# Experts in quarters of 32 slots, residual ahead of the last weights, tail two tiles ahead: one mixer and MoE layer on one core

## The chip, the cores and the metric

The kernel runs on one core of one Trainium2 chip. The metric is device time in microseconds (us). The kernel before takes 887.61 us, the median of three runs (886.54 to 891.98). Engines are named PE (matrix multiplication), DVE (vector), ACT (activation), POOL (which also issues the gathers and scatters) and SP (which issues the plain loads and stores).

## The reference

One layer: a token mixer (a state-space branch and a convolution branch), then a mixture of 32 experts, of which each of the 512 tokens takes two, then a last norm. The change touches the experts and the end.

```python
D_MODEL, SEQ, N_EXPERTS, TOP_K, D_EXPERT = 1024, 512, 32, 2, 256
...
weights = jax.nn.softmax(top_logits, axis=-1) * p_group          # two experts for a token
gate = jnp.sum(jax.nn.one_hot(expert_id, N_EXPERTS) * weights[..., None], axis=1)
out = jnp.zeros_like(h)
for e in range(N_EXPERTS):
    act = jax.nn.silu(h @ w_gate[e]) * (h @ w_up[e])             # 512x1024 @ 1024x256, twice
    out = out + gate[:, e:e + 1] * (act @ w_down[e])             # 512x256 @ 256x1024
...
x = x + gt2 * out
return rmsnorm(x, g_final)
```

## The kernel before

Until 561 us the kernel runs the mixer and the router. What the router leaves are index tables: for each expert up to 128 slots with the rows of its tokens, and the class of its size (16, 32, 48, 64, 96 or 128 slots, `SIZES`). The inputs are fixed, and so are the counts. Worked out from the reference, 20 of the 32 experts have at most 32 tokens ("small" below), 8 have 33 to 64 (11, 12, 13, 22, 24, 25, 28, 30: "middle"), and 4 have more (8, 9, 14, 15: "big").

**Expert by expert.** For each expert POOL gathers its rows (L1318) out of DRAM into `xg`, PE turns them (`tile_x`, L1329) into `st`, multiplies them by the gate and up weights (`tile_gu`, L1346, result `peg`), ACT and DVE form silu(gate) times up (`tile_act`, `sge`), PE turns that (`tile_at`, L1358, `pat`), ACT copies it (`at`), PE multiplies it by the down weights (`tile_down`, L1366, `ped`), DVE scales it by `gt2` into `ye` (`tile_y`, L1376; two buffers, used in turn), and POOL scatters `ye` to DRAM rows `ybuf` (`scatter_h`, L1401).

**Two column tiles.** Slots are worked in halves of 64, and gate and up lie on two column tiles of the array, 64 columns each: the gate of slots in partitions 0 to 63 and up in 64 to 127. The second half of the slots stands behind an If (`halves`) that is taken where the expert has more than 64 tokens. So a small or middle expert has 32 matmuls of 128x256 for gate and up and 8 of 128x512 for down, and a big one 64 and 16, as the trace counts them (two for each matmul in the code).

**Order.** The order on PE, ACT and DVE is that of the code. Step e of the loop issues on PE: gate and up of e, the turn `pat` of e-1, the turn `pxt` of the rows of e+1, down of e-1. Then DVE forms y of e-1 and POOL scatters it. POOL's order is set by the scheduler: gather of e+4, scatter of e, gather of e+5, and so on.

**Scatters.** A scatter of an expert is declared free of the scatters of the experts before it, which write other rows:

```python
    ins = halves(more[e], lambda a: scatter_h(e, a, y))
    for i_ in ins:
        for p_ in scattered:
            tc.declare_no_dep(...)          # reason="rows of different experts"
    scattered.extend(ins)
```

Nothing is declared between the scatters of one expert, so the second half's waits until the first's has landed.

**Weights.** SP loads 1 MB thirds of an expert (gate, up, down; `load_p`, `part_load`) through a ring of 20 pieces, and the loop asks for them six to seven experts ahead. Behind the last weights come the residual `x1` (2 MB) and the last gain (`last_loads`, L1507 and L1510).

**The end.** Experts 30 and 31 aren't scattered: their results are brought to the token rows by one-hot matmuls (`last_own`, L1581). The other results come back from `ybuf` (`yr`, L1565). For each of four tiles of 128 tokens `last_mix` weighs the two rows of a token (ACT, then DVE, L1586) and adds them on PE (L1588) to the residual that `last_x` (L1574) put there; then come the sum of squares on ACT, the root, the last norm on DVE (L1603) and the store. `last_mix` runs one tile ahead of the norm.

Of the kernel before, what the change touches and what calls it, by code (L numbers as in the profile page):

```python
# [2 lines left out]

# [23 lines left out]
def hybrid_kernel(  # L27
# [1240 lines left out]
    def indices(pt, p, n, name):  # L1268

        em = mz2.tile([128, 2, n], F32, tag="ixe", name=name + "_e", bufs=1)[0:p]  # L1270
        t = mz2.tile([128, 2, n], F32, tag="ixs", name=name + "_s", bufs=1)[0:p]
        V.tensor_copy(t, pt)
        V.tensor_scalar(em[:, 0], t[:, 0], 0.0, BIG, op0=ALU.is_equal, op1=ALU.mult)
        V.scalar_tensor_tensor(em[:, 1], t[:, 1], 128.0, t[:, 0], op0=ALU.mult, op1=ALU.add)
        V.scalar_tensor_tensor(em[:, 1], em[:, 0], -1.0, em[:, 1], op0=ALU.add, op1=ALU.add)
        ix = mz2.tile([p, 2, n], I32, tag="ix" + name, name=name)
        V.tensor_copy(ix[:, 1], em[:, 1])
        V.tensor_scalar(em[:, 0], em[:, 1], float(L), -float(L), op0=ALU.is_ge, op1=ALU.mult)
        V.tensor_tensor(ix[:, 0], em[:, 0], em[:, 1], op=ALU.add)
        if name == "tb":  # L1280

            pq = ps_tp("pixh")
            for a in range(2):
                for c in range(2):
                    T.matmul(pq[64 * c:64 * c + 64, n * a:n * a + n], lhsT=ident[:, 64 * a:64 * a + 64], rhs=em[:, 1], start=True, stop=True, skip_group_check=True)
            V.tensor_scalar(ixh.rearrange("p a e -> p (a e)"), pq[:, 0:2 * n], 2.0, cofs, op0=ALU.mult, op1=ALU.add)
        return ix

    ixh = mz2.tile([128, 2, NE], I32, name="ixh")
    pt = ps_tp("ptab")  # L1290
    n = 0
# [48 lines left out]

    H = [slice(64 * c, 64 * c + 64) for c in range(2)]

    def tile_gu(pg, st, r, a):
        for k in range(KD):
            for c in range(2):
                T.matmul(pg[H[c], 256 * a:256 * a + 256], lhsT=st[:, k, H[a]], rhs=r[c][k // 4][:, 256 * (k % 4):256 * (k % 4) + 256], start=(k == 0), stop=(k == KD - 1), skip_group_check=True)  # L1346

    def tile_act(pg):
        sg = mo.tile([128, 512], F32, tag="sge", name="sge", bufs=2)
        S.activation(sg[64:128], pg[0:64], AF.Silu)  # L1350
        V.tensor_tensor(sg[64:128], pg[64:128], sg[64:128], op=ALU.mult)
        return sg

    def tile_at(sg):
        pa = ps_tp("pat")[:, 0:256]
        for k in range(2):
            for a in range(2):
                T.transpose(pa[:, 128 * k + 64 * a:128 * k + 64 * a + 64], sg[64:128, 256 * a + k:256 * a + 256:2], ident[64:128, 64:128])  # L1358
# [4 lines left out]
    def tile_down(pd, at, r, a):  # L1363
        for k in range(2):
# [7 lines left out]
    def tile_y(pd):  # L1372

        y = new_y()
        for a in range(2):
            V.tensor_tensor(y[:, 512 * a:512 * a + 512], pd[a], gt2h, op=ALU.mult)  # L1376
        return y
# [22 lines left out]
    def scatter_h(e, a, y):  # L1400
        return G.indirect_dma_start(out=ybuf.rearrange("r (c n) -> (r c) n", c=2), out_offset=bass.IndirectOffsetOnAxis(ap=ixh[:, a, e:e + 1], axis=0),  # L1401
                                    in_=y[:, 512 * a:512 * a + 512], in_offset=None, bounds_check=4 * L - 1, oob_is_err=False)
# [8 lines left out]
    def scatter_e(e, y):  # L1411
        ins = halves(more[e], lambda a: scatter_h(e, a, y))
# [12 lines left out]
    with tc.If(n_gen > 0):  # L1425
        with tc.For_i(0, n_gen, 1):
# [56 lines left out]
            sg = mo.tile([128, 512], F32, tag="sge", name="sge", bufs=2)[:, 0:256]  # L1483
# [12 lines left out]
            yg = new_y()  # L1496
            for h in range(2):
                V.tensor_tensor(yg[:, 512 * h:512 * h + 512], pd[h], gt2[:, 512 * h:512 * h + 512], op=ALU.mult)
# [5 lines left out]
    def last_loads():  # L1504
        for h in range(2):
            t = eraw("x1").rearrange("p (i d) -> p i d", i=2)
            SY.dma_start(out=t, in_=x1d[256 * h:256 * h + 256].rearrange("(i p) d -> p i d", p=128))  # L1507
            x1s.append(t)
        x1s.append(eraw("gfin")[:, 0:1024])
        SY.dma_start(out=x1s[2], in_=g_final.rearrange("(o d) -> o d", o=1).to_broadcast([128, D]))  # L1510
# [34 lines left out]
    def last_y(pd, j):  # L1545

        y, parts = new_y(), eraw("yp").bitcast(F32R)
        g_ = last["gs"][:, j:j + 1]
# [27 lines left out]
    def last_own(j, parts):  # L1576

        for i in range(NT):
# [4 lines left out]
    def last_mix(i):  # L1583
        y = yrs[i][:, 0]
        S.activation(y, y, AF.Copy, scale=pw[:, i, 0:1])
        V.scalar_tensor_tensor(y, yrs[i][:, 1], pw[:, i, 1:2], y, op0=ALU.mult, op1=ALU.add)  # L1586
        for h in range(2):
            T.matmul(fin[i][h], lhsT=ident, rhs=y[:, 512 * h:512 * h + 512], start=False, stop=True, skip_group_check=True)  # L1588
# [25 lines left out]
    pgs = [ps_s5(f"peg{i}") for i in range(2)]  # L1614
    pd = [ps_mm(f"ped{i}") for i in range(2)]
    fin[0] = [ps_mm(f"fin{i}") for i in range(2)]
    with tc.manual_schedule(engines=MAN):
        for t in pgs + pd:
            V.memset(t, 0.0)
# [8 lines left out]
        for e in range(NE + 1):  # L1628
            gather_e(e + NXG)
            if e == NE - 3:  # L1630
                last_loads()
            if e > 0:
                sg = tile_act(pgs[(e - 1) % 2])
            if e < NE:
                halves(wide[e], lambda a: tile_gu(pgs[e % 2], st[e], eraws[e], a))
            load_wide(e + 1)
            if e == NE:
                last_x(0)
            if e > 0:
                at = tile_at(sg)  # L1640
            if e == NE:
                fin[1], fin[2] = pgs, [ps_tp(f"fin2{i}") for i in range(2)]
                last_x(1)
                last_x(2)
                last["y", 0] = last_y(pd, 0)
# [6 lines left out]
            if e > 0:  # L1652
                halves(wide[e - 1], lambda a: tile_down(pd, at, eraws[e - 1], a))
            if 0 < e < NE - 1:
# [16 lines left out]
        fin[3] = pd  # L1671
        last_x(3)
        for j in range(2):
            last_own(j, last["y", j])
        last_mix(0)
        for i in range(NT):
            if i + 1 < NT:
                last_mix(i + 1)
# [35 lines left out]
```

## Time and profile before

| | |
|---|---|
| median of 3 runs | 887.61 us (886.54 to 891.98) |
| the profiled execution | 891.78 us, of it a span of 890.1 |
| mixer and router | to 561 us |
| experts | 561 to 840 us (gate and up of expert 31 begin at 839.56) |
| end | from there to 890.1 us |
| granted clock of PE, mean | 0.943 |

The profile is of one execution. All durations below come from it, and it was 4.2 us slower than the median. Its time was 1.7 us above its span.

### The profile page before, as it was taken

Reading aid. Unit: us, or ns where it says so; the run is one execution under the profiler, and the core shown is the slowest. Engines: PE = TensorE matmul, PEld = TensorE weight load, DVE = VectorE, ACT = ScalarE, POOL = GpSimd, SP = SyncE. Lnnn points to the kernel's source line nnn. Section 1 sums busy time; section 2 is a strip of 40 time slices with the busy share of each in tenths; the row PEclk is TensorE's granted clock in tenths of the full one; section 3 lists DMA queues with packets and bytes.
Section 4 is the critical chain, followed back from the end, with each engine's and each line's share of the span. In section 5 each row is a group of like instructions: output and inputs, shape, how many; then the busy total and the mean of one; then the engine's idle time right before and its main releaser. Section 6 shows DMA issues by size and latency. Waiting matters only on the chain. (4 is left out here: it accounts for less than half of the span.)

```text
span 890.1 us, 14314 instructions
## 1 busy us (share of the span) xinstructions
PE 746.9 (84%) x5486; PEld 519.6 (58%) x5486; DVE 465.8 (52%) x723; ACT 321.7 (36%) x559; POOL 331.7 (37%) x293
## 2 busy tenths in 40 slices
PE   3598976988889997779999993788998988888895
PEld 0476853665566775646778872455655655555542
DVE  4948464564387797826875576133223123233254
ACT  3443611353555766637732330222112112212133
POOL 4657435343576788631610122122123122122400
PEclk9998996998988999999999996799999999999997
DMA  8926860341145546478687447999989998997042
GB/s 310 263 61 177 206 214 20 107 125 30 57 135 172 169 129 182 130 248 303 210 299 274 151 132 313 397 380 364 377 321 388 407 350 342 387 389 261 27 178 94
DMA packets 84678, 202.01 MB, mean 227 GB/s; under 512 B 12859, under 2 KB 42621, under 8 KB 74866
## 3 DMA queue, kind: packets, MB, share of 16 engines
q1 hardware_dynamic: 76754, 180.00, 57.3%
q0 software_dynamic: 5856, 12.45, 4.0%
q10 hardware_dynamic: 1984, 8.44, 3.5%
q8 instruction: 53, 0.87, 0.4%
q14 instruction: 31, 0.25, 0.1%
HBM read 180.16 MB, written 26.69 MB: 232 GB/s over the span
## 5 line engine op out<-in xcount | busy, mean ns | idle before, releaser
L1346 PE MATMUL peg<-eraw,st 128*64 128x256 f32 x1152 | 133.7, 386 | 9.5 <-PEq L1407 7.4
L1346 PEld LDWEIGHTS peg<-eraw,st 128*64 128x64 f32 x1152 | 94.7, 139 | 60.4 <-issue 34.8
L1331 DVE COPY st<-pxt 128x512 f32<-128x512 f32 x32 | 22.1, 692 | 160.0 <-PE pxt L1329 160.0
L1360 ACT ACTIVATE at<-pat 128x256 f32<-128x256 f32 x32 | 12.3, 384 | 215.8 <-PE pat L1358 215.8
L1318 POOL DMA_INDIRECT xg<-h2d,tb x32 | 30.4, 950 | 141.3 <-PE pxt L1329 129.6
L396 PE MATMUL zp<-hh,zuwh 128*128 128x512 f32 x192 | 78.7, 410 | 0.0
L398 PE MATMUL zp<-hh,zuwl 128*128 128x512 f32 x192 | 77.1, 401 | 0.5 <-POOL zuwl L752 0.3
L397 PE MATMUL zp<-hl,zuwh 128*128 128x512 f32 x192 | 76.8, 400 | 0.0
L1366 PE MATMUL ped<-eraw,at 128*64 128x512 f32 x288 | 68.9, 603 | 0.0
L98 POOL TENSOR_TENSOR adacc<-adacc,wa 128x512 f32<-128x512 f32 x30 | 47.1, 1570 | 39.9 <-ACT wa L854 37.6
L1376 DVE TENSOR_TENSOR ye<-ped,gt2h 128x512 f32<-128x512 f32 x60 | 39.0, 687 | 40.2 <-PE ped L1366 37.3
L1401 POOL DMA_INDIRECT ybuf<-ye,ixh x34 | 34.0, 999 | 69.5 <-DVE ye L1376 49.8
L1329 PE MATMUL pxt<-ident,xg 128*128 128x128 f32 x256 | 42.4, 303 | 8.1 <-DMA xg<-h2d,tb 7.4
L396 PEld LDWEIGHTS zp<-hh,zuwh 128*128 128x128 f32 x192 | 37.4, 195 | 11.9 <-issue 4.4
L398 PEld LDWEIGHTS zp<-hh,zuwl 128*128 128x128 f32 x192 | 37.2, 194 | 9.8 <-POOL zuwl L752 1.8
L397 PEld LDWEIGHTS zp<-hl,zuwh 128*128 128x128 f32 x192 | 37.1, 193 | 7.4
L1329 PEld LDWEIGHTS pxt<-ident,xg 128*128 128x128 f32 x256 | 33.6, 194 | 13.1 <-issue 8.6
L1358 PE MATMUL pat<-ident,sge 64*128 64x64 f32 x128 | 21.3, 286 | 18.9 <-PEq L1407 18.2
L1358 PEld LDWEIGHTS pat<-ident,sge 64*128 64x128 f32 x128 | 17.7, 209 | 32.7 <-PEq L1407 30.4
L1366 PEld LDWEIGHTS ped<-eraw,at 128*64 128x64 f32 x288 | 17.8, 136 | 27.2 <-issue 23.6
L98 POOL TENSOR_TENSOR vb<-vta,vtb 128x512 f32<-128x512 f32 x16 | 22.3, 1393 | 30.0 <-PE pv L533 19.1
L752 DVE TENSOR_TENSOR zuwl<-zr,zuwh 128x1024 fp32r<-128x1024 f32 x16 | 28.4, 1775 | 5.7 <-ACT zuwh L751 5.6
(494 smaller groups left out, 1666.9 us busy)
## 6 DMA issues: line engine op xcount, KB each, us to landing
eraw<-in_w_exp_gate_dram SPq DMA_DIRECT2D x24, 1024.0 KB
eraw<-in_w_exp_up_dram SPq DMA_DIRECT2D x24, 1024.0 KB
eraw<-in_w_exp_down_dram SPq DMA_DIRECT2D x24, 1024.0 KB
wa<-in_w_ada_dram SPq DMA_DIRECT2D x32, 512.0 KB
zr<-in_w_in_dram SPq DMA_DIRECT2D x12, 1024.0 KB
wa<-in_w_ada_dram SPq DMA_DIRECT2D x8, 1024.0 KB
eraw<-in_w_exp_gate_dram SPq DMA_DIRECT2D x14, 512.0 KB
eraw<-in_w_exp_down_dram SPq DMA_DIRECT2D x14, 512.0 KB
```

The costliest lines, as they stand in the source:

```text
L98: G.tensor_tensor(o, a, b, op=op)
L396: T.matmul(acc, lhsT=wh, rhs=ah, start=start, stop=False)
L397: T.matmul(acc, lhsT=wh, rhs=al, start=False, stop=False)
L398: T.matmul(acc, lhsT=wl, rhs=ah, start=False, stop=stop)
L752: (G if t in ZPOOL else V).tensor_tensor(zu[t][1], raw, zu[t][0].bitcast(F32), op=ALU.subtract)
L1318: G.indirect_dma_start(out=xg, out_offset=None, in_=h2d, in_offset=bass.IndirectOffsetOnAxis(ap=idx, axis=0), bounds_check=L - 1, oob_is_e ...
L1329: T.transpose(pt[:, k, :], xg[:, 4 * h + k:D:8], ident)
L1346: T.matmul(pg[H[c], 256 * a:256 * a + 256], lhsT=st[:, k, H[a]], rhs=r[c][k // 4][:, 256 * (k % 4):256 * (k % 4) + 256], start=(k == 0), s ...
L1358: T.transpose(pa[:, 128 * k + 64 * a:128 * k + 64 * a + 64], sg[64:128, 256 * a + k:256 * a + 256:2], ident[64:128, 64:128])
L1366: T.matmul(pd[a][H[c]], lhsT=at[:, 128 * k + 64 * a:128 * k + 64 * a + 64], rhs=r[2][k][:, 512 * c:512 * c + 512], start=(k == 0), stop=(k ...
L1376: V.tensor_tensor(y[:, 512 * a:512 * a + 512], pd[a], gt2h, op=ALU.mult)
L1401: return G.indirect_dma_start(out=ybuf.rearrange("r (c n) -> (r c) n", c=2), out_offset=bass.IndirectOffsetOnAxis(ap=ixh[:, a, e:e + 1], a ...
```

## The change

- **Quarters.** Slots are worked in quarters of 32. Gate and up lie on four column tiles of 32 columns: the gate of row block k, up of k, gate of k+1, up of k+1. The two partial sums of each are added afterwards. So `tile_act` has two copies on ACT and two additions on DVE ahead of two silus and two multiplications. `pat` is eight turns in place of four, and down is four column tiles of 256 columns. Two Ifs stand in place of one (`quarters`): the second quarter where an expert has more than 32 tokens, the third and fourth where it has more than 64. `peg` takes four banks, two for each expert of a pair.
- **Scatters.** Four scatters of 256 columns (`scatter_q`) stand in place of two of 512, with an index table of 4 columns for an expert (`ixq`).
- **Loads.** `x1`, the last gain and the halves of `gt2` are loaded ahead of the weights of expert 31. A quarter-wide copy of `gt2` stays on the chip through the experts.
- **The end.** Down of experts 30 and 31 stays in halves (`tile_down_h`). `last_x` of tiles 1 and 2 stands behind it, `last_own` does tiles 0 to 2 first, and `last_mix` runs two tiles ahead, apart from the addition on PE (`last_add`).

```diff
+    loads = [partial(third, m) for m in range(93)] + [lambda: load_x1(0), lambda: load_x1(1), lambda: load_gain()]
+    loads += [partial(third, m) for m in range(93, 96)]
...
+    Q = [slice(32 * c, 32 * c + 32) for c in range(4)]
     H = [slice(64 * c, 64 * c + 64) for c in range(2)]
+    B4 = [(a // 2, slice(256 * (a % 2), 256 * (a % 2) + 256)) for a in range(4)]

     def tile_gu(pg, st, r, a):
-        for k in range(KD):
-            for c in range(2):
-                T.matmul(pg[H[c], 256 * a:256 * a + 256], lhsT=st[:, k, H[a]], rhs=r[c][k // 4][:, 256 * (k % 4):256 * (k % 4) + 256], start=(k == 0), stop=(k == KD - 1), skip_group_check=True)
+        b, cs_ = B4[a]
+        for k2 in range(0, KD, 2):
+            for c in range(4):
+                k = k2 + c // 2
+                T.matmul(pg[b][Q[c], cs_], lhsT=st[:, k, Q[a]], rhs=r[c % 2][k // 4][:, 256 * (k % 4):256 * (k % 4) + 256], start=(k2 == 0), stop=(k2 == KD - 2), skip_group_check=True)

     def tile_act(pg):
-        sg = mo.tile([128, 512], F32, tag="sge", name="sge", bufs=2)
-        S.activation(sg[64:128], pg[0:64], AF.Silu)
-        V.tensor_tensor(sg[64:128], pg[64:128], sg[64:128], op=ALU.mult)
+        t = mo.tile([128, 1024], F32, tag="sga", name="sga", bufs=1)
+        sg = mo.tile([128, 1024], F32, tag="sge", name="sge", bufs=1)
+        hs = [slice(0, 512), slice(512, 1024)]
+        for b in range(2):
+            S.activation(t[0:64, hs[b]], pg[b][64:128], AF.Copy)
+        for b in range(2):
+            V.tensor_tensor(t[0:64, hs[b]], pg[b][0:64], t[0:64, hs[b]], op=ALU.add)
+            S.activation(sg[32:64, hs[b]], t[0:32, hs[b]], AF.Silu)
+        for b in range(2):
+            V.tensor_tensor(sg[32:64, hs[b]], t[32:64, hs[b]], sg[32:64, hs[b]], op=ALU.mult)
         return sg
...
+    def quarters(size_, f):
+
+        r = [f(0)]
+        with tc.If(size_ > SIZES.index(32)):
+            r.append(f(1))
+        with tc.If(size_ > SIZES.index(64)):
+            r += [f(2), f(3)]
+        return r
...
     def scatter_e(e, y):
-        ins = halves(more[e], lambda a: scatter_h(e, a, y))
+        ins = quarters(more[e], lambda a: scatter_q(e, a, y))
...
+        last_mix(0)
+        last_mix(1)
         for i in range(NT):
-            if i + 1 < NT:
-                last_mix(i + 1)
+            last_add(i)
+            if i + 2 < NT:
+                last_mix(i + 2)
             last_sum(i)
```

What this does to the order of instructions is shown at three places. On PE, down of one expert and the start of gate and up of the next; `ped` and `peg` are the results, `eraw` the weights. Before:

```order
L1366 MATMUL ped_5159<-eraw,at 64x512 [waits DMAHW5_49]
L1387 UNCONDITIONAL_BRANCH
L1366 MATMUL ped_5159<-eraw,at 64x512 x3
L1407 COMPARE_AND_BRANCH
L1366 MATMUL ped_5160<-eraw,at 64x512 x4
L1407 UNCONDITIONAL_BRANCH
L1407 UNCONDITIONAL_BRANCH [waits PE_49]
L1346 MATMUL peg_5158<-eraw,st 64x256 [waits DMAHW2_49,Activation_49]
```

The same place now:

```order
L1395 MATMUL ped_5177<-eraw,at 32x256 [waits DMAHW4_49]
L1424 UNCONDITIONAL_BRANCH
L1395 MATMUL ped_5177<-eraw,at 32x256 x7
L1444 COMPARE_AND_BRANCH
L1395 MATMUL ped_5177<-eraw,at 32x256 x8
L1444 UNCONDITIONAL_BRANCH
L1444 UNCONDITIONAL_BRANCH [waits PE_49]
L1446 COMPARE_AND_BRANCH
L1395 MATMUL ped_5178<-eraw,at 32x256 x16
L1446 UNCONDITIONAL_BRANCH
L1446 UNCONDITIONAL_BRANCH [waits PE_49]
```

A small expert now runs the first 8 matmuls (16 as the trace counts them), each of 32 columns by 256, and skips two Ifs instead of one; each If ends in a branch that waits for PE.

On POOL, the scatters of one expert; `DMASW` are the counters of landed transfers of POOL's queue. Before:

```order
L1401 DMA ybuf<-ye,ixh 2048x512 [waits DMASW0_49,DVE_49]
L1407 COMPARE_AND_BRANCH
L1401 DMA ybuf<-ye,ixh 2048x512 [waits DMASW0_49,DVE_49]
L1407 UNCONDITIONAL_BRANCH
L1407 ISA [waits DMASW1_49]
```

And now:

```order
L1438 DMA ybuf<-ye,ixq 4096x256 [waits DMASW2_49,DVE_49]
L1444 UNCONDITIONAL_BRANCH
L1446 UNCONDITIONAL_BRANCH
L1444 COMPARE_AND_BRANCH
L1438 DMA ybuf<-ye,ixq 4096x256 [waits DMASW3_49,DMASW2_49]
L1444 UNCONDITIONAL_BRANCH
L1444 ISA [waits DMASW3_49]
L1444 UNCONDITIONAL_BRANCH
L1446 COMPARE_AND_BRANCH
L1438 DMA ybuf<-ye,ixq 4096x256 [waits DMASW3_49,DMASW4_49,DMASW2_49,DVE_49]
L1438 DMA ybuf<-ye,ixq 4096x256 [waits DMASW5_49,DMASW4_49]
```

Each of the four scatters of an expert waits for the landing of the one before it. A big expert had one such wait and has three, a middle one had none and has one.

On DVE, from one expert's y to the next multiplication ahead of `pat`. Before:

```order
L1376 TENSOR_TENSOR ye<-ped_5159,gt2h 128x512 [waits DMASW0_49,DMASW1_49,DVE_49,PE_49]
L1376 TENSOR_TENSOR ye<-ped_5160,gt2h 128x512 [waits PE_49]
L1351 TENSOR_TENSOR sge<-peg_5157,sge 64x512 [waits Activation_49]
L1407 UNCONDITIONAL_BRANCH x2
L1387 UNCONDITIONAL_BRANCH
L1331 COPY st<-pxt 128x512 [waits DVE_49,PE_49]
```

And now:

```order
L1412 TENSOR_TENSOR ye<-ped_5177,gt2q 128x512 [waits DMASW6_49,DMASW5_49,DMASW7_49,DMASW0_49,PE_49]
L1412 TENSOR_TENSOR ye<-ped_5178,gt2q 128x512 [waits PE_49]
L1376 TENSOR_TENSOR sga<-peg_5175,sga 64x512 [waits Activation_49]
L1444 UNCONDITIONAL_BRANCH
L1446 UNCONDITIONAL_BRANCH
L1376 TENSOR_TENSOR sga<-peg_5176,sga 64x512 [waits Activation_49]
L1379 TENSOR_TENSOR sge<-sga,sge 32x512 [waits Activation_49]
L1444 UNCONDITIONAL_BRANCH
L1446 UNCONDITIONAL_BRANCH
L1379 TENSOR_TENSOR sge<-sga,sge 32x512 [waits Activation_49]
```

The first y waits for the landing of all scatters that read this `ye` buffer last, four counters in place of two, and two additions and a second multiplication stand behind it.

## Rows read from the trace of the kernel before

**Rows 1.** The page: the span and the busy time of each engine.

```profile
span 890.1 us, 14314 instructions
PE 746.9 (84%) x5486; PEld 519.6 (58%) x5486; DVE 465.8 (52%) x723; ACT 321.7 (36%) x559; POOL 331.7 (37%) x293
```

**Rows 2.** Windows (from:to, length, busy (count) by engine, PEclk, DMA share, GB/s).

```profile
560.00:655.00 95.00, 85.27 (x603) 54.15 (x603) 27.91 (x51) 20.99 (x35) 20.04 (x21) 0.96 0.97 366
650.00:655.00 5.00, 5.00 (x36) 2.32 (x34) 2.27 (x4) 0.12 (x1) 1.71 (x2) 1.00 0.49 129
815.00:840.00 25.00, 21.97 (x156) 13.86 (x154) 7.67 (x13) 4.71 (x9) 9.61 (x10) 1.00 0.11 35
```

**Rows 3.** Timeline of PE: start, duration, instruction, in brackets idle before and releaser.

```profile
640.49 7.13 PE L1346 MATMUL peg<-eraw,st 128*64 128x256 f32 x64 [0.31 <-PEq L1407]
...
649.40 3.65 PE L1366 MATMUL ped<-eraw,at 128*64 128x512 f32 x16
...
729.62 3.67 PE L1346 MATMUL peg<-eraw,st 128*64 128x256 f32 x32 [0.31 <-PEq L1407]
734.01 0.66 PE L1358 MATMUL pat<-ident,sge 64*128 64x64 f32 x4 [0.71 <-PEq L1407]
734.60 1.31 PE L1329 MATMUL pxt<-ident,xg 128*128 128x128 f32 x8
735.84 1.94 PE L1366 MATMUL ped<-eraw,at 128*64 128x512 f32 x8
738.09 3.67 PE L1346 MATMUL peg<-eraw,st 128*64 128x256 f32 x32 [0.31 <-PEq L1407]
...
839.56 3.67 PE L1346 MATMUL peg<-eraw,st 128*64 128x256 f32 x32 [0.31 <-PEq L1407]
```

**Rows 4.** Timeline of PE, other stages: matmuls on 32 columns.

```profile
59.77 1.07 PE L259 MATMUL pm<-wa,condz 128*32 128x256 f32 x16
...
396.50 0.64 PE L845 MATMUL pma<-wa,condz 128*32 128x256 f32 x8 [0.69 <-DMA wa<-in_w_ada_dram]
```

**Rows 5.** Timelines of ACT and DVE around a small expert.

```profile
735.97 0.59 ACT L1350 ACTIVATE sge<-peg 64x512 f32<-64x512 f32 x1
...
738.25 1.29 DVE L1376 TENSOR_TENSOR ye<-ped,gt2h 128x512 f32<-128x512 f32 x2 [1.62 <-DMA ybuf<-ye,ixh]
739.57 0.69 DVE L1351 TENSOR_TENSOR sge<-peg,sge 64x512 f32<-64x512 f32 x1
```

**Rows 6.** Timeline of POOL: both scatters of experts 8, 9 and 15.

```profile
652.36 1.00 POOL L1401 DMA_INDIRECT ybuf<-ye,ixh  x1 [1.64 <-DVE ye L1376]
657.96 0.98 POOL L1401 DMA_INDIRECT ybuf<-ye,ixh  x1 [4.60 <-DMA ybuf<-ye,ixh]
...
662.02 1.00 POOL L1401 DMA_INDIRECT ybuf<-ye,ixh  x1 [1.63 <-DVE ye L1376]
670.23 0.98 POOL L1401 DMA_INDIRECT ybuf<-ye,ixh  x1 [7.22 <-DVE st L1331]
...
721.36 1.00 POOL L1401 DMA_INDIRECT ybuf<-ye,ixh  x1 [0.31 <-issue]
730.11 0.98 POOL L1401 DMA_INDIRECT ybuf<-ye,ixh  x1 [7.76 <-DVE ye L1376]
```

**Rows 7.** The tile ybuf: its scatters, and the time from issue to landing.

```profile
L1401 POOL DMA_INDIRECT ybuf<-ye,ixh x34: 969/999/1047, 579.2 to 841.0; - x34
...
DMA to landing us min/median/max: 2.3/7.2/9.6
```

**Rows 8.** Timeline of PE at the end: the additions of tiles 0, 2 and 3.

```profile
870.12 1.88 PE L1588 MATMUL fin<-yr,ident 128*128 128x512 f32 x4
...
876.14 2.58 PE L1588 MATMUL fin<-yr,ident 128*128 128x512 f32 x4 [2.42 <-DVE yr L1586]
879.37 3.78 PE L1588 MATMUL ped<-yr,ident 128*128 128x512 f32 x4 [0.65 <-DVE yr L1586]
```

**Rows 9.** Windows of PE: length, PE busy (count), PEclk, DMA share, GB/s.

```profile
857.00:858.00 1.00, 0.31 (x2) 1.00 0.00 0
861.00:862.00 1.00, 1.00 (x3) 0.50 0.00 0
864.00:865.00 1.00, 1.00 (x6) 1.00 0.00 0
```

More of the change, by code (lines that the diff above doesn't have):

```diff
@@ L1280, in indices @@
         if name == "tb":
-            pq = ps_tp("pixh")
-            for a in range(2):
-                for c in range(2):
-                    T.matmul(pq[64 * c:64 * c + 64, n * a:n * a + n], lhsT=ident[:, 64 * a:64 * a + 64], rhs=em[:, 1], start=True, stop=True, skip_group_check=True)
-            V.tensor_scalar(ixh.rearrange("p a e -> p (a e)"), pq[:, 0:2 * n], 2.0, cofs, op0=ALU.mult, op1=ALU.add)
+            pq = ps_tp("pixq")
+            for a in range(4):
+                for c in range(4):
+                    T.matmul(pq[32 * c:32 * c + 32, n * a:n * a + n], lhsT=ident[:, 32 * a:32 * a + 32], rhs=em[:, 1], start=True, stop=True, skip_group_check=True)
+            V.tensor_scalar(ixq.rearrange("p a e -> p (a e)"), pq[:, 0:4 * n], 4.0, cofs, op0=ALU.mult, op1=ALU.add)
         return ix
-    ixh = mz2.tile([128, 2, NE], I32, name="ixh")
+    ixq = mz2.tile([128, 4, NE], I32, name="ixq")
     pt = ps_tp("ptab")
@@ L1363, in tile_down, with tile_down_h @@
     def tile_down(pd, at, r, a):
+        b, cs_ = B4[a]
+        for k in range(2):
+            for c in range(4):
+                T.matmul(pd[b][Q[c], cs_], lhsT=at[:, 128 * k + 32 * a:128 * k + 32 * a + 32], rhs=r[2][k][:, 256 * c:256 * c + 256],
+                         start=(k == 0), stop=(k == 1), skip_group_check=True)
+    def tile_down_h(pd, at, r, a):
         for k in range(2):
@@ L1502, in hybrid_kernel, with load_x1, load_gain @@
     x1s = []
[L1504 to L1510, printed above, removed]
+    def load_x1(h):
+        t = eraw("x1").rearrange("p (i d) -> p i d", i=2)
+        SY.dma_start(out=t, in_=x1d[256 * h:256 * h + 256].rearrange("(i p) d -> p i d", p=128))
+        x1s.append(t)
+    def load_gain():
+        t = eraw("gfin")
+        SY.dma_start(out=t[:, 0:1024], in_=g_final.rearrange("(o d) -> o d", o=1).to_broadcast([128, D]))
+        gate2(t[:, 1024:1536], 2)
+        x1s.extend([t[:, 0:1024], t[:, 1024:1536]])
     DIRECT = (NE - 2, NE - 1)
@@ L1574, in last_x, with last_own @@
             T.matmul(fin[i][h], lhsT=ident, rhs=xis[i][:, 512 * h:512 * h + 512], start=True, stop=False, skip_group_check=True)
-    def last_own(j, parts):
-        for i in range(NT):
+    def last_own(j, ts, parts):
+        for i in ts:
             for r_ in parts:
@@ L1651, in hybrid_kernel @@
                 last_turn(0)
-            if e > 0:
-                halves(wide[e - 1], lambda a: tile_down(pd, at, eraws[e - 1], a))
-            if 0 < e < NE - 1:
+            if e == NE:
+                last["y", 0] = last_y(pd, 0)
+            if e >= NE - 1:
+                tile_down_h(pd, at, eraws[e - 1], 0)
+                with tc.If(wide[e - 1] > SIZES.index(64)):
+                    tile_down_h(pd, at, eraws[e - 1], 1)
+            elif e > 0:
+                quarters(wide[e - 1], lambda a: tile_down(pd, at, eraws[e - 1], a))
                 scatter_e(e - 1, tile_y(pd))
@@ L1670, in hybrid_kernel @@
         S.activation(rs2, rs2, AF.Sqrt)
-        fin[3] = pd
+        fin[1], fin[2], fin[3] = pgs[1], [ps_tp(f"fin2{i}") for i in range(2)], pd
+        last_x(1)
+        last_x(2)
+        for j in range(2):
+            last_own(j, range(3), last["y", j])
         last_x(3)
         for j in range(2):
-            last_own(j, last["y", j])
+            last_own(j, range(3, NT), last["y", j])
         last_mix(0)
+        last_mix(1)
         for i in range(NT):
-            if i + 1 < NT:
-                last_mix(i + 1)
+            last_add(i)
+            if i + 2 < NT:
+                last_mix(i + 2)
             last_sum(i)
```

69 lines of the change are left out of this document (36 added, 33 removed).

## The prediction

> **What bounds the kernel now.** I read the span first [rows 1], then the windows of the expert stage, then the timelines of PE, of POOL and of the end. The change works between 561 us and the end. In the windows PE is busy 85.27 of 95 us at clock 0.96, and the DMA engines are busy too, at 0.97 and 366 GB/s [rows 2]. Which of the two binds? From 815 us to 840 the DMA share is 0.11: the last load was in some 24 us before gate and up of expert 31 began at 839.56 [rows 2, 3]. So the loads lead and PE sets the pace. The timeline of PE shows how: a small expert takes 8.47 us (729.62 to 738.09), made of gate and up 3.67, a gap of 0.71 at the skipped If, `pat` 0.59, `pxt` 1.24, down 1.94 and a gap of 0.31 [rows 3]. What could bind in PE's place is POOL's chain of scatters: the second of a big expert stood 5.60, 8.21 and 8.75 us behind the first [rows 6], about the landing time, whose median is 7.2 [rows 7]. The first of these names the landing as what it waited for. The others name pieces of DVE work that hold nothing the scatter reads, but the order of POOL has the same wait for the first half's transfer in all. And y waits once, 1.62 us, for scatters to land before it may reuse its buffer, right behind the pair 14 and 15 [rows 5].
>
> **PE, a small expert.** A quarter of gate and up is 32 matmuls on 32 columns as the trace counts them (two for each one in the order). Of that form the trace has 16 in 1.07 us and 8 in 0.64 [rows 4], so (1.07 - 0.64)/8 = 0.054 us each, and 1.07 + 16 x 0.054 = 1.93 us a quarter, against 3.67 [rows 3]. The gap of 0.71 stays, and for the second skipped If I add another like the one after down, 0.31 (0 to 0.71). That is 2.95 for 4.38: -1.43. A quarter of down is 16 of the same form, 1.07 us, with 0.31 more for its second If: 1.69 for 2.25, -0.56. Eight turns for four double `pat` to 1.18: +0.59, for small, middle and big alike. Middle and big experts win nothing else: two quarters make 1.93 + 32 x 0.054 = 3.65 and four 7.1, as 3.67 and 7.13 now, and down the same [rows 3]. Sum: 20 x -1.43, 19 x -0.56 (expert 31's down stays in halves) and 31 x 0.59: -28.6 - 10.6 + 18.3 = -20.9.
>
> **ACT and DVE.** The new chain from one down to the next is two y (1.29), two additions from PSUM (0.69 each, the price of the multiplication of 64x512 now), a silu (0.59), the last multiplication (0.69) [rows 5], then eight turns (1.18), `pxt` (1.24; the copy of `at` lies under it) and down (1.07): 7.4 us. PE's own sum is 2.95 + 1.18 + 1.24 + 1.69 = 7.06. So between small experts PE waits about 0.35; over some 14 such neighbours that is +5 (0 if the multiplications of 32x512 are short, +10 if the copies on ACT join the chain). So far -16.
>
> [...]
>
> **The scatters.** The scatters of one expert wait for each other's landing, and the change makes three such waits of one for a big expert, and one of none for a middle one. Take the pitch between them as 7.5, the mean of 5.60, 8.21 and 8.75, and the landing as 7.2 [rows 6, 7]. Put y of expert 8 at 0. Its scatters go at 0, 7.5, 15 and 22.5; the last lands at 29.7. POOL is one queue, so the next gather (1 us) and the first scatter of 9 come behind it, at 24.5, the others to 47, landed at 54.2. On DVE y(10) reuses the buffer of y(8), y(11) that of y(9). By PE's pace they would come at 17.5 and 26.5: a step is 9.0 (10's gate and up 2.95, turns 2.42, 9's down 3.65), then 8.5 and 9.0 likewise. So y(10) is 12 late and y(11) 27 in all. Behind y in DVE's queue stand the additions and multiplications of the next expert, so its `pat`, and PE, stand too. It is the same for 14 and 15 with 16 and 17. At a pitch of 5.60 and a landing of 4.7 the same sum gives 14, at 8.75 and 8.2 it gives 36. A middle expert's two scatters, 7.5 + 7.2, are landed within its two steps of 17 and cost nothing. I take 15 a pair, near the low end: when PE stands the ring of weights fills and loads stop, and the one short pitch is the one that began where the DMA share was 0.49 [rows 2, 6]. [...] I add 2 a pair (0 to 4). Together +34, bounds 28 and 62 (two pairs at 27, and 8 for the clock; 36 would need loads that go on through the stall).
>
> **Loads and index tables.** The residual, the gain and the halves of `gt2` are 2.75 MB, 7 us at 366 GB/s, now ahead of expert 31's weights. These would land at about 816 where `x1` did, and even at -16 gate and up of 31 begin at 823, so this costs nothing; cover gone, at most 7. The 16 small matmuls for `ixq` lie before 561 and cost under 1. The gathers share POOL's queue with the longer scatters, but each has two steps of time: 0 outside of the pairs.
>
> **The end.** Before, the additions of tiles 2 and 3 waited 2.42 and 0.65 for DVE's mix, and that of tile 3 ran 3.78 where tile 0 took 1.88 [rows 8], at half clock after the idle. Two tiles ahead the mixes are done in time: up to -2.42 - 0.65 - 1.90 = -5. The additions were not all on the path, since norms and stores follow; I take -4 (0 to -5). The moved `last_x` and `last_own` are the same matmuls in another order: 0.
>
> **Sum**, against the profiled execution: 891.78 - 16 + 34 - 4 = 905.8. It was 4.2 above the median of its runs, so on their footing 901.6, say **902**. With bounds: 28 gives 896, 62 gives 930.
>
> **Rivals.**
>
> (a) *Scatters land fast; the gain stands.* The shortest landing is 2.3 [rows 7], and a quarter moves half the bytes of a half. At a landing of 2.3 and 1 us of issue a pitch is 3.3: 8's go to 9.9, 9's from 11.9 to 21.8, landed at 24.1, before y(11) at 26.5. No stall: 891.78 - 16 - 4 - 4.2 = 867.6, **868**. It decides where the pitch falls below some 4. For it: transfers are smaller and PE's stalls empty the queues. Against: the median over the stage is 7.2 while the loads run, and single-scatter experts of few rows are in it. 0.17.
>
> [...]
>
> (b) *A wash.* Only the first scatter of a burst lands slowly; once PE stands, the ring fills and the rest land in 2.3 to 4.7. Then a pair costs about 8: 891.78 - 16 + 16 - 4 - 4.2 = 883.6, **884** (880 to 892). For it: the 5.60 of the first pair. Against: POOL's pitch stayed at 8.2 and 8.75 right behind [rows 6]. 0.18.
>
> (c) *The four column tiles don't overlap* as the rows on 32 columns do, which come from other stages with other weights. Were a matmul on 32 columns as long as one on 64 now (3.67/32 = 0.115), a quarter would cost 3.67, a small expert gain 0 on gate and up, lose 0.31 + 0.59 + 0.31 = 1.2, a middle one 3.67 + 0.59 + 1.9 = 6.2 and a big one twice as much less 0.59: 24 + 50 + 47 = +121, so **1000** with the end's -4 and no stalls. The rows speak against it: 0.05.
>
> **How the numbers follow.** The forecast, stalls of 25 to 62, has 0.60 and covers 893 to 930. Runs of this kernel can tell about 1% from no change, that is 878.7 to 896.5. Of the forecast's 0.60 some 0.07 lies under 896.5. So: faster 0.19 (rival a, and a little of b), same 0.23 (b and the forecast's lower edge), slower 0.58. The range 868 to 922 leaves out half of (a), (c) and the forecast's upper edge.
>
> **What would show it.** Right: gate and up of a small expert 1.9 to 2.0 us in 32 matmuls; periods of 7.1 to 7.5 among small experts; four scatters of 8, 9, 14 and 15 some 5 to 8 us apart; y of 10, 11, 16 and 17 idle before it with `ybuf` as releaser, 30 us in all; gate and up of 31 at 850 to 865; the end 4 us shorter. Wrong: y never waits on `ybuf` (rival a), pitches fall to 3 after the first (b), or a quarter takes 3.7 (c). A period over 8 among small experts would mean that ACT and DVE bind more than summed, and the forecast would be too low.

## The result, and the profile after

The changed kernel takes 955.46 us, the median of four runs (949.0 to 962.33), against 888.64 before: 1.0749 times the time before, 95% interval 1.0664 to 1.0835. The profiled execution has a span of 959.7 us where that of before had 890.1 [rows 1], and its time, 962.33, stands 7 us above the median of its runs.

Gate and up of expert 31 begin at 910.8 us instead of 839.56 [rows 3]. From there to the end it is 48.9 us instead of 50.5. The whole loss, 71 us, lies among the experts, where the forecast had 18.

Here is the page of the changed kernel: the span, the granted clock of PE in 40 slices, and one row of the queues.

```profile
span 959.7 us, 17075 instructions
...
PEclk9998979999989999999999766679779875878989
...
q8 instruction: 82, 1.34, 0.6%
```

The same row of the queues before:

```profile
q8 instruction: 53, 0.87, 0.4%
```

From slice 23 on (a slice is 24 us), where the experts work, most digits of the clock row are 5 to 8; before, the windows there had 0.96 to 1.00 [rows 2]. The transfers of program code (q8; their number, then MB) are 82, where before there were 53.

The next rows are windows of the changed kernel (from:to, length, busy and count of PE, PEld, DVE, ACT and POOL, PEclk, DMA share, GB/s). The first holds the small experts ahead of the first big one, the second the remainder of the experts.

```profile
571.00:640.00 69.00, 52.50 (x414) 28.84 (x413) 29.31 (x56) 24.56 (x43) 12.68 (x13) 0.65 0.90 334
640.00:910.00 270.00, 204.50 (x2416) 128.73 (x2416) 102.99 (x161) 75.44 (x138) 66.10 (x67) 0.81 0.70 257
```

At 0.65 some 70% of the first stretch ran at half clock (0.35 of 0.50), taking the clock as either whole or half: in 56 of the 62 windows of 0.5 us from 600 to 631 it was 1.00 or 0.50. This is before the first big expert and so before any chain of scatters. The timeline of PE in that stretch shows a small expert's step:

```profile
600.15 3.64 PE L1366 MATMUL peg<-eraw,st 128*32 128x256 f32 x32 [0.75 <-PEq L1446]
605.15 1.11 PE L1386 MATMUL pat<-ident,sge 32*128 32x32 f32 x8 [1.35 <-PEq L1446]
606.19 1.31 PE L1344 MATMUL pxt<-ident,xg 128*128 128x128 f32 x8
607.43 1.94 PE L1395 MATMUL ped<-eraw,at 128*32 128x256 f32 x16
610.66 3.64 PE L1366 MATMUL peg<-eraw,st 128*32 128x256 f32 x32 [1.29 <-PEq L1446]
```

Gate and up take 3.64, twice the 1.93 that the forecast had, and down 1.94 for 1.07: each matmul at half the clock, which was 0.50 from 600 to 603.5 us and from 607.5 to 611. `pat` and `pxt` between them run at the full one, 1.00 from 604 to 607. The gaps are 1.35 and 1.29 where before they were 0.71 and 0.31 [rows 3]. The step takes 10.5 us, and over the four steps to 630.62 it is 10.1 on average, against 8.47 before and 7.4 in the forecast. Of what the step shown lies over the forecast's own sum for PE, the slower gate and up and down make 2.6 us (1.71 + 0.87) and the longer gaps 1.0 (2.64 for 1.02 + 0.62). Late in the same execution a step ran at full clock, 1.00 in each us from 890 to 899:

```profile
890.06 1.11 PE L1386 MATMUL pat<-ident,sge 32*128 32x32 f32 x8 [0.71 <-PEq L1446]
...
892.35 1.07 PE L1395 MATMUL ped<-eraw,at 128*32 128x256 f32 x16
894.67 1.93 PE L1366 MATMUL peg<-eraw,st 128*32 128x256 f32 x32 [1.25 <-PEq L1446]
897.74 1.16 PE L1386 MATMUL pat<-ident,sge 32*128 32x32 f32 x8 [1.14 <-DVE sge L1379]
```

There gate and up are the forecast's 1.93 and down its 1.07, but from `pat` to `pat` it is still 7.7.

The forecast's stalls are there too. First POOL's four scatters of expert 8, then DVE's y of experts 10, 11, 16 and 17, then the landing times of the tile ybuf:

```profile
667.18 1.00 POOL L1438 DMA_INDIRECT ybuf<-ye,ixq  x1 [1.67 <-DVE ye L1412]
669.89 0.99 POOL L1438 DMA_INDIRECT ybuf<-ye,ixq  x1 [1.70 <-DMA ybuf<-ye,ixq]
677.18 0.98 POOL L1438 DMA_INDIRECT ybuf<-ye,ixq  x1 [6.30 <-DMA ybuf<-ye,ixq]
685.21 0.97 POOL L1438 DMA_INDIRECT ybuf<-ye,ixq  x1 [7.05 <-DMA ybuf<-ye,ixq]
```

```profile
689.96 1.29 DVE L1412 TENSOR_TENSOR ye<-ped,gt2q 128x512 f32<-128x512 f32 x2 [3.25 <-DMA ybuf<-ye,ixq]
...
713.02 1.29 DVE L1412 TENSOR_TENSOR ye<-ped,gt2q 128x512 f32<-128x512 f32 x2 [13.96 <-DMA ybuf<-ye,ixq]
...
771.56 1.29 DVE L1412 TENSOR_TENSOR ye<-ped,gt2q 128x512 f32<-128x512 f32 x2 [4.46 <-DMA ybuf<-ye,ixq]
...
791.06 1.29 DVE L1412 TENSOR_TENSOR ye<-ped,gt2q 128x512 f32<-128x512 f32 x2 [12.04 <-DMA ybuf<-ye,ixq]
```

```profile
DMA to landing us min/median/max: 2.1/5.3/7.7
```

Each scatter after the first names the one before it as what it waited for, and y stood 3.25 + 13.96 + 4.46 + 12.04 = 33.7 us in the four places that the forecast named. So the stalls came as forecast, and something else cost as much again. This is what PE waited for, in all (us, times, longest):

```profile
PE pat L1386 <- DVE sge L1379: 36.2, 9, 12.2
PE pat L1386 <- PEq L1446: 24.9, 17, 4.5
PE peg L1366 <- PEq L1446: 21.0, 24, 2.1
```

And before:

```profile
PE pat L1358 <- PEq L1407: 18.2, 26, 0.8
PE peg L1346 <- PEq L1407: 7.4, 24, 0.3
```

Of the first row 25.7 us are three waits behind the stalls of y (12.24, 9.82 and 3.67); the others are waits for the chain over ACT and DVE. The other two rows of the changed kernel are gaps at Ifs, 45.9 us, where the like before came to 25.6.

### The profile page after: what moved, and what is told of

It reads as the page before. It is cut to its first block, busy times and chain, and to the rows that moved or that the text cites. A ratio compares the mean times of both kernels' runs of the same rounds, so it can differ in the third digit from the quotient of the medians.

```text
span 959.7 us, 17075 instructions
## 1 busy us (share of the span) xinstructions
PE 759.5 (79%) x6662; PEld 522.8 (54%) x6662; DVE 524.8 (55%) x821; ACT 376.3 (39%) x655; POOL 345.1 (36%) x308
## 5 line engine op out<-in xcount | busy, mean ns | idle before, releaser
L1366 PE MATMUL peg<-eraw,st 128*32 128x256 f32 x1648 | 123.5, 456 | 22.6 <-PEq L1446 20.3
L1366 PEld LDWEIGHTS peg<-eraw,st 128*32 128x32 f32 x1648 | 67.4, 128 | 78.3 <-issue 59.4
L1438 POOL DMA_INDIRECT ybuf<-ye,ixq x49 | 48.8, 996 | 130.5 <-DMA ybuf<-ye,ixq 83.2
L1386 PE MATMUL pat<-ident,sge 32*128 32x32 f32 x256 | 37.2, 284 | 64.9 <-DVE sge L1379 37.2
L1377 ACT ACTIVATE sge<-sga 32x512 f32<-32x512 f32 x64 | 39.2, 629 | 123.5 <-DVE sga L1376 101.7
L1412 DVE TENSOR_TENSOR ye<-ped,gt2q 128x512 f32<-128x512 f32 x60 | 39.4, 688 | 77.1 <-DMA ybuf<-ye,ixq 33.7
L1386 PEld LDWEIGHTS pat<-ident,sge 32*128 32x128 f32 x256 | 33.6, 209 | 84.2 <-PEq L1446 45.8
L1395 PE MATMUL ped<-eraw,at 128*32 128x256 f32 x784 | 65.7, 485 | 0.0
L1379 DVE TENSOR_TENSOR sge<-sga,sge 32x512 f32<-32x512 f32 x64 | 41.1, 679 | 4.2 <-ACT sge L1377 1.1
L1376 DVE TENSOR_TENSOR sga<-peg,sga 64x512 f32<-64x512 f32 x64 | 40.7, 674 | 0.5 <-ACT sga L1374 0.5
```

Source lines behind the costliest of these rows:

```text
L1366: T.matmul(pg[b][Q[c], cs_], lhsT=st[:, k, Q[a]], rhs=r[c % 2][k // 4][:, 256 * (k % 4):256 * (k % 4) + 256], start=(k2 == 0), stop=(k2 == ...
L1376: V.tensor_tensor(t[0:64, hs[b]], pg[b][0:64], t[0:64, hs[b]], op=ALU.add)
L1379: V.tensor_tensor(sg[32:64, hs[b]], t[32:64, hs[b]], sg[32:64, hs[b]], op=ALU.mult)
L1386: T.transpose(pa[:, 128 * k + 32 * a:128 * k + 32 * a + 32], sg[32:64, 256 * a + k:256 * a + 256:2], ident[32:64, 32:64])
L1395: T.matmul(pd[b][Q[c], cs_], lhsT=at[:, 128 * k + 32 * a:128 * k + 32 * a + 32], rhs=r[2][k][:, 256 * c:256 * c + 256], start=(k == 0), st ...
L1412: V.tensor_tensor(y[:, 512 * b:512 * b + 512].rearrange("p (a n) -> p a n", a=2), pd[b].rearrange("p (a n) -> p a n", a=2), gt2q.unsqueeze ...
```

## The experiments

Three theories stood at first. **S**: the chain of scatters is the loss. **I**: the second skipped If is. **C**: the quarters leave PE so little work in a step that its clock falls, stalls or not. The first four runs took one suspect each.

**Independent scatters.**

```diff
-        for i_ in ins:
-            for p_ in scattered:
+        for k_, i_ in enumerate(ins):
+            for p_ in scattered + ins[:k_]:
```

> The changed kernel with the scatters of one expert declared independent of each other. Theory S (the loss is the chain of scatters): the 34 us that y stood for ybuf are gone, and with them every half-clock stretch that a stall started; the time falls by 34 to 60, to 895 to 921. Theory C (the loss is the clock, which falls for want of work on PE between the skipped Ifs, scatters or not): the stalls go, but small experts stay at 10 us a step with 3.6 us for gate and up, since 571 to 640 us was like that before the first big expert; 918 to 930, still clearly slower than before.

Measured: 944.04 us, 1.0591 times before (1.0555 to 1.0626). Nobody waited on ybuf any more, yet only 11 us were won. The time lies above both ranges: S alone isn't the loss, and C was too low. The waits of PE moved to the Ifs:

```profile
PE pat L1386 <- PEq L1446: 48.6, 22, 4.7
...
PE pat L1386 <- DVE sge L1379: 5.5, 4, 1.9
```

The 48.6 holds gaps of a size that the kernel before never had. From the timeline of the same run:

```profile
571.54 1.11 PE L1386 MATMUL pat<-ident,sge 32*128 32x32 f32 x8 [3.03 <-PEq L1446]
...
585.38 1.13 PE L1386 MATMUL pat<-ident,sge 32*128 32x32 f32 x8 [4.58 <-PEq L1446]
...
638.16 1.14 PE L1386 MATMUL pat<-ident,sge 32*128 32x32 f32 x8 [3.53 <-PEq L1446]
```

There are nine gaps at Ifs over 2.5 us in this run and two in the changed kernel; that the stalls cover them there is an inference.

**One skipped If instead of two.**

```diff
         with tc.If(size_ > SIZES.index(32)):
             r.append(f(1))
-        with tc.If(size_ > SIZES.index(64)):
-            r += [f(2), f(3)]
+            with tc.If(size_ > SIZES.index(64)):
+                r += [f(2), f(3)]
```

> The changed kernel with the second If inside the first, so that a small expert skips one If on PE and POOL instead of two. Theory I (the added skipped If is what costs): the gap ahead of gate and up of a small expert falls from 0.74 to 1.3 to about 0.3, that ahead of pat by some 0.5, and the clock comes back to 1.00 among small experts: 20 x (0.9 + up to 2.5), 890 to 935. Theory C without the Ifs (PE has too little work in a step however it is skipped): gaps shrink by about 0.5 each, 15 to 20 us, but gate and up of small experts stay at 3.6; 935 to 942.

Measured: 947.7 us, 1.063 (1.0584 to 1.0676), 8 less than the changed kernel, but the two intervals overlap, and the time lies above both ranges. The gap ahead of gate and up shrank as theory I has it, but gaps of 2.5 to 6 us ahead of `pat` remained, with 82 transfers of code. So the number of skips isn't the main thing.

**No Ifs on PE.** The quarters of an expert are written out from its known count.

```diff
-            quarters(wide[e], lambda a: tile_gu(pgs[e % 2], st[e], eraws[e], a))
+            fixed(e, lambda a: tile_gu(pgs[e % 2], st[e], eraws[e], a))
```

> The changed kernel with no If on PE at all: the quarters of each expert are written out from its known count (right for these inputs only); POOL keeps its Ifs. Theory I: without gaps the clock stays at 1.00, a small step is bound by ACT and DVE at about 7.4, and only the scatter stalls of some 34 us are left: 890 to 905. Theory C: PE still stands 2 us of a 7.4 us step and its matmuls are narrow, so gate and up stay at 3.6 in the small stretches, a step is 8 to 8.5, 915 to 930.

Measured: 919.66 us, 1.0319 (1.028 to 1.0357). The Ifs are worth 36 us here. All gaps at PEq are gone, code transfers are back at 53, y still stands 33.9 for ybuf. The clock is between 0.70 and 0.81 in the first three windows of 20 us, so theory I's full clock didn't come; the time is theory C's.

**A second If in the kernel before.**

```diff
         r = [f(0)]
+        with tc.If(size_ > len(SIZES) - 1):
+            f(0)
         with tc.If(size_ > SIZES.index(64)):
```

> The kernel before with a second If, never taken, ahead of the one on gate and up and on down. Theory I: the gaps are 0.4 to 0.6 longer twice a step, +25 to +35 for 31 experts, and the clock falls to half in the stretches of small experts as it did in the changed kernel, another +30 or more: 915 to 960. Rival (the narrow tiles, not the gaps, take the clock): the gaps alone, 905 to 925, the granted clock stays at 1.00.

Measured: 924.83 us, 1.0386 (1.0358 to 1.0415), which lies in both ranges. The granted clock decides: it was 0.95 from 571 to 640 us and 0.99 from 640 to 840, so mostly at full. The rows show the gaps, and the first one a down that took 3.33 for 1.94:

```profile
597.57 3.33 PE L1366 MATMUL ped<-eraw,at 128*64 128x512 f32 x8
601.62 3.67 PE L1346 MATMUL peg<-eraw,st 128*64 128x256 f32 x32 [0.72 <-PEq L1416]
606.42 0.66 PE L1358 MATMUL pat<-ident,sge 64*128 64x64 f32 x4 [1.13 <-PEq L1416]
```

Each skip adds 0.41 to 0.42 (0.72 for 0.31 and 1.13 for 0.71), which over 31 steps with two of them is 26 of the 34 us. Among the experts from 570 us on the clock fell in three places only, each time for one down (3.52, 3.33 and 3.45 for 1.94), 4.5 us more; the last 3 to 4 aren't accounted for. So the gaps took little of the clock while PE worked on 64 columns, and the rival holds but for that.

**Both away.** Of the next four runs the first two take both suspects away, the others go on with one. Independent scatters and no If on PE:

> The changed kernel with both taken away: scatters of one expert independent, and no If on PE (quarters written out from the known counts). Theory I+S (skipped Ifs and scatter stalls are the whole loss): a small step is bound by ACT and DVE at 7.4 and the clock is 1.00, 875 to 885. Theory C (the quarters leave PE too little to do, and the clock falls without stalls and gaps): gate and up of small experts still 2 to 3.6 us, steps of 8 and more, 890 to 905.

Measured: 885.1 us, 0.995 (0.9911 to 0.9989). Against the run without Ifs, the scatters are worth 35 us, which is the forecast's size; with the Ifs in place only 11 of it showed in the first run. The time is at the upper edge of I+S and 5 under C's range, but the clock, and a step of 8.2 us on average from 580.71 to 621.52, are C's. With neither stall nor If the quarters are hardly ahead of the kernel before. The window of the small experts says why:

```profile
571.00:640.00 69.00, 58.37 (x668) 36.13 (x660) 35.72 (x66) 26.80 (x48) 14.69 (x15) 0.82 1.02 394
```

**The same with work that nobody reads, to hold up the clock**: 8 matmuls of 128x128 ahead of each `pat`.

```diff
+        for _ in range(8):
+            T.matmul(pf[:, 256:384], lhsT=ident, rhs=ident, start=True, stop=True, skip_group_check=True)
```

> The same with 8 more matmuls of 128x128 (16 as the trace counts them), whose result nobody reads, ahead of each expert's pat, where PE waits 1.2 to 1.9 us for DVE. Theory C: PE's work holds the clock at 1.00 and the step falls to the 7.4 of the ACT and DVE chain, 10 to 25 us under the run without the filling, though PE does more. Rival (clock and wait have nothing to do with each other, the chain binds): no gain, or up to 20 slower since the filling takes PE longer than the wait.

Measured: 894.0 us, 1.0032 (0.9994 to 1.0069): 9 slower, which is the rival's figure. The clock did come up, to 0.97 to 1.00 between 600 and 820 us, and small steps to 7.7; but the filling cost its 2 us in middle and big experts too, where PE has no wait to put it in. This run joined two effects and settled little by its time.

**A long body behind the second If.**

> The kernel before with a second If, never taken, as in the run with one, but with three times the matmuls inside, so that PE's program is about as long as the changed kernel's. Theory L (the skipped code is loaded): instruction transfers rise from 54 to about 80, gaps of 2.5 to 6 us stand behind some skips, 935 to 960. Rival (a skip costs the same however long the code): like the run with the short one, 922 to 928, 54 transfers.

Measured: 927.32 us, 1.0433 (1.0346 to 1.052), 54 transfers. It is a miss: nothing changed against the short body, in the transfers or in the 14381 instructions that the two traces count. The likely reason is that the sizes are stated to be at most 5, so the compiler left the body out of both runs and both have the bare If; the run with 6 stated, below, bears this out.

**Gate and up alone in quarters**, in the kernel before, with the sums, silus and turns that belong to them:

> The kernel before with quarters for gate and up alone (two Ifs there); down, scatters, loads and end are as before. Theory C+L: the clock holds longer, since down still works on 64 columns (1.94 at full clock), the gap behind gate and up is 2 us in place of 0.7 and eats the 1.74 that the quarter saves, a step is 8.5 to 9.5 and some skips wait 3 us and more: 890 to 925. Rival (all the loss is in down and its scatters): 875 to 885.

Measured: 1.0459 times before (1.0375 to 1.0544), 71 transfers of code. Worse than expected: this part alone, with its Ifs, loses 41 us.

**Down and scatters alone in quarters**, with loads and end as changed:

> The changed kernel with gate and up, the activation and its turn as before (halves on 64 columns, one If); down and scatters stay in quarters, loads and end as changed. Theory C (gate and up in quarters take the clock, by the gaps and the two more stages on ACT and DVE): the clock is back at 1.00 among small experts, a step is 8.0 to 8.3, and what is left over before is the scatter stalls and a second skip on down: 895 to 920. Rival (down in quarters does it as well): half clock among small experts, 930 to 950.

Measured: 911.67 us, 1.0267 (1.0216 to 1.0318), waits for DVE of 22.5 us that come from the scatters, steps of 8.1, and this clock among the small experts:

```profile
571.00:640.00 69.00, 57.60 (x531) 41.14 (x527) 23.34 (x45) 15.34 (x27) 15.59 (x16) 1.00 1.02 393
```

These are theory C's figures. So 41 us are gate and up's and 21 down's with its scatters (the loads and the end give some back), which make 62 of the 67.

**The body behind the If, really there.** The largest size is stated as 6.

```diff
-            f(0)
+            for _ in range(3):
+                f(0)
...
-min_val=0, max_val=len(SIZES) - 1,
+min_val=0, max_val=len(SIZES),
```

> The kernel before with a second If, never taken, as in the runs with one, but with a largest size stated as 6, so that the compiler can't drop its body: three times the matmuls of the first half stand in the program and are skipped (in the two runs before they weren't there). Theory L (skipped code is loaded): instruction transfers rise from 54 to about 80, gaps of 2.5 to 6 us stand behind some skips, 935 to 965. Rival (a skip costs the same with or without code behind it): 922 to 930, 54 transfers, no gap above 1.5.

Measured: 955.96 us, 1.0766 (1.0707 to 1.0826): 31 us over the bare If, by code that never runs. Bare If and body together lose 65 us, about as much as the whole change. Timeline and queue of this run:

```profile
594.97 0.71 PE L1358 MATMUL pat<-ident,sge 64*128 64x64 f32 x4 [3.54 <-PEq L1417]
...
597.51 3.32 PE L1366 MATMUL ped<-eraw,at 128*64 128x512 f32 x8
```

```profile
q8 instruction: 84, 1.38, 0.6%
```

Transfers rise from 54 to 84, eleven waits of 1.5 to 3.7 us stand in the experts, and behind ten of them `pxt` or down ran at half clock, as here down with 3.32 for 1.94 (with the bare If that was so in three places). The waits are shorter than theory L's 2.5 to 6, but the time and the transfers are its own: L holds, for this kernel. In the changed kernel it is shown by less, by 82 transfers with the Ifs and 53 without, and by the long gaps that go with them.

**The other two parts of the change alone**, loads and end, in the kernel before:

> The kernel before with the two other parts of the change alone: residual and gain loaded ahead of expert 31's weights, and the new order of the end with the mix two tiles ahead. By the trace of the changed kernel, where gate and up of 31 to the end took 48.9 for 50.5: 1 to 2 us faster. By the prediction's term: 4 faster. Rival (loads ahead delay the last weights): same or up to 5 slower.

Measured: 885.01 us, 0.9954 (0.9925 to 0.9983), so 4 faster, the prediction's term and not the 1 to 2 that the changed kernel's trace gave. In its trace gate and up of 31 begin at 836.21 and the span is this:

```profile
span 880.2 us, 14316 instructions
```

That is 44.0 from there to the end, in this one execution, for 50.5 before. **With independent scatters** as well:

> The same with the two scatters of a big expert declared independent. Where y waited once, 1.62 us, in the kernel before: 1 to 2 us faster than that; rival (PE never waited for them): no difference.

Measured: 884.58 us, 0.995 (0.9923 to 0.9978): no difference, as the rival has it. These two are half a percent faster than the kernel before, and unlike the runs without Ifs they suit any routing.

**Halves without Ifs.** What was still open is whether the quarters are worth anything in themselves.

> The kernel before without any If on PE: its halves are written out from the known counts (right for these inputs only). Its gaps of 0.71 and 0.31 a step, 25 us by the waits, go. If the quarters are no gain in themselves, it is clearly under the changed kernel without Ifs and stalls (885): 862 to 870, a small step 7.4 to 7.5 at clock 1.00. If the quarters gain and only the Ifs eat it: 885 or more, since the gaps hid something else.

Measured: 860.48 us, 0.9684 (0.9629 to 0.9739). This is a little under what was expected. The halves' own Ifs cost 30 us, with the code behind them (44 transfers without, 53 with), and without them a small step is 7.19, at full clock:

```profile
597.67 3.62 PE L1346 MATMUL peg<-eraw,st 128*64 128x256 f32 x32
601.23 0.69 PE L1358 MATMUL pat<-ident,sge 64*128 64x64 f32 x4
601.84 1.31 PE L1329 MATMUL pxt<-ident,xg 128*128 128x128 f32 x8
603.09 1.94 PE L1366 MATMUL ped<-eraw,at 128*64 128x512 f32 x8
604.86 3.62 PE L1346 MATMUL peg<-eraw,st 128*64 128x256 f32 x32
```

**Quarters without Ifs and stalls, with the clock held up in small experts alone:**

```diff
-                at = tile_at(sg)
+                at = tile_at(sg, 8 if e < NE and CNT[e] <= 32 else 0)
```

> The changed kernel without Ifs on PE and with independent scatters, with the 8 unread matmuls ahead of pat only where the expert whose gate and up came just before has at most 32 tokens. Theory C: clock 1.00, small steps of 7.7 in place of 8.5, some 10 to 16 under the run without filling: 868 to 876. Rival (the way over ACT and DVE binds whatever the clock): 882 to 890.

Measured: 862.73 us, 0.9713 (0.9655 to 0.977). It is 22 us faster than the run without the filling, with more work on PE, and better than theory C expected. Its clock among the small experts, where the run without had 0.82, and its timeline:

```profile
571.00:640.00 69.00, 66.94 (x848) 47.96 (x847) 38.02 (x62) 28.46 (x51) 17.60 (x18) 0.98 1.02 391
```

```profile
592.51 1.91 PE L1366 MATMUL peg<-eraw,st 128*32 128x256 f32 x32
594.35 2.05 PE L1385 MATMUL pat<-ident 128*128 128x128 f32 x16
596.34 1.24 PE L1389 MATMUL pat<-ident,sge 32*128 32x32 f32 x8
597.51 1.31 PE L1344 MATMUL pxt<-ident,xg 128*128 128x128 f32 x8
598.75 1.07 PE L1398 MATMUL ped<-eraw,at 128*32 128x256 f32 x16
599.64 1.91 PE L1366 MATMUL peg<-eraw,st 128*32 128x256 f32 x32
```

A step is 7.13 and PE never stands in it. Theory C holds: holding the clock up was worth 22 us, net of what the filling takes. And quarters (862.73, the 4 us of loads and end included) are no faster than halves (860.48) even so, since what their shorter matmuls save (1.91 + 1.07 for 3.62 + 1.94) goes to the longer turn (1.24 for 0.69) and to the filling, or without it to the wait for ACT and DVE.

## Why the prediction was wrong

It forecast slower and got it, but 902 (868 to 922) is 53 short of 955. Laid out by the runs, from halves without any If (860): quarters with the clock held up 863, without 885 (clock, +22), with the chain of scatters 920 (+35), with the Ifs 955 (+36). Taken in the other order the Ifs are 59 (885 to 944) and the scatters 11 (944 to 955), so the two overlap. The kernel before is the same 860 with its own Ifs, 890. The sign was forecast for the stalls, which came; most of the loss has another cause.

- **What bounds: right in part.** PE set the pace, and loads did not bind: PE waited 2.0 us for weights in all. But by the prediction's own sums PE, at 7.06, was no longer full under a chain of 7.4, and it drew nothing from that but a wait of 0.35.
- **PE, a small expert: the step that failed.** The prediction gave gate and up with their gaps 2.95 and down 1.69, and the step 7.4; in the first stretch of small experts it was 10.1. Two of its terms were wrong. "For the second skipped If I add another like the one after down, 0.31 (0 to 0.71)" took a skip as a price of its own. A bare one costs 0.42 and lies within the bounds. The code behind it had no term: in the kernel before it came to 31 us for a body that never ran, about as much as the bare Ifs' 34. And the quarter's 1.93 and 1.07 were put in for every step, without a word on the clock. So they are at full clock; in that stretch the clock was 0.65 and they took 3.64 and 1.94. Without Ifs and stalls the clock was still 0.82, and with PE's waits filled 0.98 and 22 us less.
- **ACT and DVE: a little high.** With the clock held up a step is 7.13 in place of 7.4. That this chain binds where PE gets faster was right: without Ifs and stalls `pat` waited for it 20 times, 29.9 us in all. The sign that was named for it, a period over 8, came too, but for another reason: the gaps of such a step are at the Ifs, and its matmuls ran at half clock.
- **The scatters: right in place and mechanism, and in size only where no Ifs hide them.** The forecast was 30 for y and 4 for the clock; y stood 33.7 at 10, 11, 16 and 17, and the runs with and without the chain differ by 35 without Ifs on PE. In the changed kernel itself, with its Ifs, taking the chain away won 11. Single pitches of the big experts ranged from 2.7 to 8.0, with the short one first and not, as forecast, last.
- **A stall costs clock: right, and far too narrow.** The prediction counted it behind the stalls only, 4 us in all. No run shows its 2 us a pair as such. In the kernel before, behind a wait of PE of 1.49 us, the clock was 0.50 from 861 to 863 us and 1.00 again from 864 [rows 9]. In the changed kernel it was 0.50 from 707 to 723 us, in and behind the one wait of 12.24; there `pat`, `pxt` and down took 1.43, 1.97 and 3.64 for 1.16, 1.31 and 1.93 at full clock, 2.6 us more. The prediction never asked what the clock would do among small experts without a stall.
- **Loads and end: right.** Alone they are 4 faster. In the changed kernel 1.6 of it show, since down of 30 and 31 ran partly at half clock (3.50 and 3.18 for 1.94).
- **The rivals.** (c) looked at the right place, the small steps, and named a wrong cause: the four column tiles do overlap, 1.93 a quarter at full clock. (a) and (b) fell: y did wait for `ybuf`, and the pitches behind the first were 5.7 to 8.0.

What would have raised the question: of a small step before, 7.4 of 8.47 are matmuls. Taking 1.74 + 0.87 of them away and adding 0.59 of turns, while gaps and chain stay, leaves 5.4 in a step that the chain holds at 7.4. What the clock does then the rows of before don't say, and it took a run to see.

## What to carry to other kernels

When PE's work in a step is cut below what the engines beside it need, little can be gained (here 863 us against 860, with the clock held up), and it can lose if the clock falls, as here to 0.82 even without Ifs and stalls (885 us); the time of the step's longest chain is to be added up before the matmuls are halved. An If that mostly skips was paid here by its branch (34 us) and by the code behind it (31 us), so the code behind Ifs belongs into the comparison of two layouts. And two losses that overlap (here stalls and code) look small when either is taken away alone; take away both before judging one.

## What the runs showed of the hardware

**Code that is skipped was paid for.** The same kernel with a skipped body of 48 + 12 matmuls a step had 84 transfers of code instead of 54, eleven waits of 1.5 to 3.7 us, and 31 us more. One transfer is 0.87 MB / 53 = 16.4 KB on average in the kernel before, and 1.38 MB / 84, as much, in this run. That the skips set off the added transfers is an inference: no row ties a transfer to a wait.

**The clock fell without a long idle.** In the changed kernel's first stretch no wait of PE among the four steps from 590 to 630 is over 1.4 us, and still gate and up took 3.64 in each, for 1.93 at full clock. The kernel before with a second bare If, with waits up to 1.26, ran every matmul between 602 and 640 at full clock, gate and up in 3.67 and down in 1.94. From 600 to 640 PE was busy 31.6 us in the one and 31.7 in the other, so the busy time of a page doesn't tell the two apart. In the changed kernel the clock went down and up within a step, 0.50 under gate and up and 1.00 under `pat` and `pxt`, and was 0.65 on average over 69 us. Why it did so no row shows, and whether the gaps or the narrow tiles weigh more wasn't separated. With gate and up alone back on 64 columns the clock was 1.00, with gaps of 0.7 to 0.9 us; with the quarters kept, filling the waits was enough: 0.98 for 0.82, and 22 us less.
